# A two-layer Hyena and SSD trunk: weight loads and fresh stores issued from ScalarE's queue from layer 1 on

## The chip, the cores and the metric

The kernel runs on one core of a Trainium2 chip. The metric is the device time of one execution in microseconds (us). TensorE (PE) does the matrix products, VectorE (DVE), ScalarE (ACT) and GpSimd (POOL) the rest; SyncE (SP) only issues DMAs. A DMA can be issued from SP's, ACT's or POOL's instruction stream, and each of these streams is carried out in order.

## The reference

The input x is 1024 steps by 1024 channels, float32. Each layer computes h = LayerNorm(sqrt(2) h + mixer(h)). Layer 0's mixer is a bidirectional Hyena convolution. Layer 1's is a bidirectional Mamba-2 scan (SSD), cut to what matters:

```python
proj = x @ w_in                                  # z 2048, x B C 3072, dt 64 columns
xbc = silu(centred_depthwise_conv(xbc, conv_w, conv_b))          # 5 taps
# forward and backward, in 4 groups of 8 heads and 8 chunks of 128 steps:
states = einsum('bcsgn,bcghs,bcsghp->bcghpn', B, decay_states, x * dt)
y = y_diag + einsum('bctgn,bcghpn,bcght->bctghp', C, prev_states, exp(a_cs))
y = rms_norm_groups(y * silu(z), norm_g, 4)
return y @ w_out                                 # 2048 x 1024
```

## The kernel before, in words

Products are made in three parts: every operand is split into a high part h and a rest l, and H.H + H.L + L.H are added up in PSUM. So every weight tile is loaded to `wr`, cast by ACT to `wh` (L214, or L217 with a gain per row), and subtracted by DVE to `wl` (L215, L218). `weights` (L206 to L219) does these three; its load, at L211, is issued from SP. There are two `wr` tiles in the pool for the whole program, so the third load waits until DVE has made `wl` of the first; in layer 0's output projection the odd rows have two more of their own.

The stages in order of time:

- Layer 0's mixer, up to some 1120 us: projections at L261, the filters' and the signal's transforms.
- Layer 0's output projection (`out_layer`, products at L1193), up to some 1285 us, in passes of 2, 3 and 3 blocks of 128 rows of time; each pass reads all 16 rows of blocks of `w_out` (512 KB each) and y from DRAM (`yr`, L1175, split to `yh` and `yl`). It begins beside the end of the mixer; its first four groups of two rows of `w_out` are emitted there.
- Layer 1's projections (`flow` in `ssd`, products at L743), 40 units of 128 channels, with one `w1` load of 512 KB each, prepared in the middle of the unit before. A unit of x, B or C goes through `conv5` (ACT at L668, DVE four times at L671, Silu by ACT at L673) to a tile `cv`, and then through `ssd_xbc`: B and C are stored as they are (L961, 8 stores), x and B are transposed by PE (L969), copied by ACT to `tr` (L971, two tiles) and stored (L974, 40 stores), all to the DRAM tensor `bxd`.
- Layer 1's scan, from some 1400 us on, beside the projections. `ssd_back` takes the chunks of a group backwards, `ssd_forth` forwards one group later. Both load a chunk of B, C and x from `bxd` to `bx` (L983, three tiles), and the decays `ec` (L1017), each row of which is spread over 64 partitions. PE's first product of a chunk is at L1043, its last that reads `bx` at L1085. `ssd_back` stores its part to `ybd` (L1091), `ssd_forth` loads that (L1109), finishes y and stores it (L1147). In the last group, `values` (L1005) puts these tiles where h1^T lay (`h1th`, `h1tl`).
- Layer 1's output projection, like layer 0's, from some 2010 us to the end. Its early groups run beside the scan's last chunks. In its passes of three blocks, eight pairs of `wh` and `wl` are held, so that casts can run ahead.

What sets the order: the source emits the work as interleaved generators (`Pipe`, `fill`, `advance`), and the tile framework then writes a list for each engine when the program is built. It takes, on each engine, the instruction that its plan finds ready and that stands first in the source, so a list is near to the source's order but not the same. On the chip every engine carries out its list in order and waits at each instruction on semaphores, a DMA issue too: for its tile to be free, for the data that it stores, and for an earlier DMA that counted on the same semaphore.

The weight load and the stores of `ssd_xbc` before the change:

```python
# weights
nc.sync.dma_start(out=wr if len(src.shape) == 2 else ..., in_=src)          # L211
nc.scalar.copy(wh, wr)
nc.vector.tensor_tensor(out=wl, in0=wr, in1=wh.bitcast(F32), op=ALU.subtract)
# ssd_xbc
nc.scalar.copy(o, ps)                                                       # o is tr
nc.sync.dma_start(out=dst[:, c, n:n + 128], in_=o)                          # L974
```

Of the kernel before, what the change touches and what calls it, by code (L numbers as in the profile page):

```python
"""Hybrid encoder trunk, two layers on one core: a bidirectional Hyena layer, then a bidirectional
Mamba-2 SSD layer, each with its DeepNorm residual.

Matrix products run on float32r operands: each float32 operand is split into a high part of 12
significant bits and the rest (x = H + L), and a product is H.H + H.L + L.H in float32 PSUM.

Hyena's long convolution is evaluated at the 1024 points z_g = exp(-2 pi i (g + 1/4) / 1024). With
z^1024 = -i the products of a real signal and a two-sided real kernel wrap into the imaginary part,
so one complex transform of length 1024 gives the linear convolution of length 2048. The transform
is two stages (64 x 16) of matrix products, with t = 16 t1 + t2 and g = g1 + 64 g2.  # L10
"""
# [16 lines left out]
L = 1024  # L28
# [60 lines left out]
def _round12(a):  # L89
    """float64 -> float32 values with 12 significant bits, nearest even."""  # L90
    m, e = np.frexp(a)
    return np.ldexp(np.rint(m * 4096.0), e - 12).astype(np.float32)
# [40 lines left out]
def _constants():  # L133
    k = {}
# [3 lines left out]
    # both parts side by side, the high one first where n2 is even  # L138
# [34 lines left out]
class Pipe:  # L173
    """Tasks under way, each a generator that yields between its stages; a step moves each by a stage."""
# [15 lines left out]
class Build:  # L190
    def __init__(self, tc, a, p, pp, dp):
        """p, pp, dp: pools in SBUF (weights' tiles), PSUM and DRAM for the whole program."""
        self.tc, self.nc, self.a, self.p, self.pp, self.dp = tc, tc.nc, a, p, pp, dp
        self.ident = p.tile([128, 128], F32, name="ident")
        self.nc.sync.dma_start(out=self.ident, in_=a["ident"])
        self.ready = lambda k: True
        self.mhalf = p.tile([128, 1], F32, name="mhalf")
        self.nc.vector.memset(self.mhalf, -0.5)
# [7 lines left out]
    def weights(self, src, gain=None, pool=None, bufs=2, name="w"):  # L206
        """128 x 1024 (or 512) weights in two parts, times a gain per row if there is one."""
# [3 lines left out]
        nc.sync.dma_start(out=wr if len(src.shape) == 2 else wr.rearrange("p (k c) -> p k c", k=src.shape[1]), in_=src)  # L211
# [10 lines left out]
    def split(self, src, h, l):  # L222
        """h + l = src, both float32r."""
        self.nc.scalar.copy(h, src)  # L224
        self.nc.vector.tensor_tensor(out=l, in0=src, in1=h.bitcast(F32), op=ALU.subtract)  # L225

    def pair(self, pool):
        """The two parts' tiles of [128, 512] values."""
        return pool.tile([128, 512], F32R, name="xh", bufs=XB), pool.tile([128, 512], F32R, name="xl", bufs=XB)

    def load_pair(self, pool, src):
        """[128, 512] values from DRAM in two parts."""
# [12 lines left out]
    def load_r(self, pool, name, shape, src):  # L245
        """A float32r tile from float32 values that have 12 significant bits."""
# [4 lines left out]
    def projections(self, work, ahead, xh, xl):  # L251
        """Projections of x^T, each [128 channels, 1024] in PSUM for its function; a step per quarter of one."""
# [17 lines left out]
    def filter_mlp(self, pm, hs):  # L270
        """The filter network's last hidden layer at 16 n1 + n2 and at 1024 - (16 n1 + n2), in two parts on top of
        each other."""
# [45 lines left out]
    def filters(self, kd, sh, t):  # L318
        """The convolution kernels' transforms, to kd[block][re/im][64][16][256]; yields the tasks of each step."""
# [3 lines left out]
        def stage2(cb, j):  # L323
            # the last of the first stage's results go to DRAM two steps after their task's first
# [17 lines left out]
        with tc.tile_pool(name="k0", bufs=1) as p:  # L342
# [5 lines left out]
            with tc.tile_pool(name="k1", bufs=1) as p:  # L348
# [19 lines left out]
                def stage1(cb, m, k):  # L368
                    """The kernels at n2 = 2 m and 2 m + 1, and their transforms' first stage."""
# [42 lines left out]
    def hyena(self, yt, after):  # L412
        """Layer 0's mixer up to its output projection: from x^T (permuted time) to y^T in DRAM."""
# [4 lines left out]
        with tc.tile_pool(name="h0", bufs=1) as p, tc.tile_pool(name="hf", bufs=1, space=PSUM) as self.pf:  # L418
# [17 lines left out]
            for n, s in (("ta", [128, 16, 128]), ("tb", [128, 128]), ("tbi", [128, 128])):  # L436
                for q in "hl":
                    t[n + q] = (pa if n + q == "tah" else p).tile(s, F32R, name=n + q)
                    flat = t[n + q].rearrange("p a b -> p (a b)") if len(s) == 3 else t[n + q]
                    if n == "ta":  # L440
                        # not before x
# [5 lines left out]
            def u_work(b):  # L447
                """x1 * v for 256 channels."""
# [9 lines left out]
            def q_work(b):  # L458
                """x0 * silu(z) for 256 channels."""
# [14 lines left out]
            def fill(n):  # L474
                """Projections up to n quarters in all."""
# [23 lines left out]
            with tc.tile_pool(name="h1", bufs=1) as pf:  # L499
# [19 lines left out]
                for i, item in enumerate(todo):  # L519
                    if tabs and i == tabs[0][0]:  # L520
                        # a table's load waits for the products under way
# [41 lines left out]
    def hyena_fft(self, sh, t, us, spill, pb2):  # L563
        """A quarter of the first stage of the transform of 256 channels, to DRAM."""
# [34 lines left out]
    def hyena_mid(self, sh, p, t, kd, b, spill, vspill, j):  # L599
        """The transform's second stage, its product with the filters', and the inverse's first, to DRAM."""  # L600
# [29 lines left out]
    def hyena_back(self, sh, p, t, yt, b, vspill, qs, gs, pb2):  # L630
        """A quarter of the inverse's second stage times qs, to yt in the order of time."""
# [44 lines left out]
    def ssd(self, h1t, wdt, yt, after):  # L676
        """Layer 1's mixer up to its output projection: from h1^T to the normed y^T in DRAM; the first steps of what
        comes after are taken beside its last chunks."""
        tc, nc, a = self.tc, self.nc, self.a
        with tc.tile_pool(name="s", bufs=1) as p, tc.tile_pool(name="sf", bufs=1, space=PSUM) as self.pf:  # L680
# [10 lines left out]
            # the exponents' factors: in each direction, rows of ones (2), of the columns' terms (16)  # L691
            # against rows of the sums (2), and of the heads' places (16); odd chunks in the lower half
# [9 lines left out]
            # whether y^T's rows k, k + 1 are in DRAM for the first blocks  # L702
# [6 lines left out]
            # B, C, B^T and x at each chunk  # L709
# [19 lines left out]
            def flow():  # L729
# [7 lines left out]
                def column(ps, w, k, halves):  # L737
                    """What one k adds to 128 channels."""
# [5 lines left out]
                # the first two go through the first half of the time, then through the second  # L744
# [33 lines left out]
            def fill(n):  # L778
                """The order's units up to n quarters in all."""
# [18 lines left out]
            with tc.tile_pool(name="sc", bufs=1) as self.ps:  # L798
# [9 lines left out]
                def places(g):  # L808
                    """The group's rows of the exponents' factors."""
# [13 lines left out]
                for n in range(4):  # L823
# [4 lines left out]
                    else:  # L828
                        # the projections' input has been read
# [26 lines left out]
    def ssd_dt(self, p, h1t, t, wdt):  # L856
        """dt, the chunks' running sums of dt * a in both directions, and what follows of them."""
# [6 lines left out]
        # the second half of the time lies below the first: 64 heads x 512 steps each  # L864
# [32 lines left out]
        def columns(src):  # L897
            """[128, 2, 4, 64]: the heads along each row of the chunks."""
# [48 lines left out]
        def spread(c):  # L947
            """The chunk's exp(running sums) to DRAM, its heads of a parity together."""
# [7 lines left out]
    def ssd_xbc(self, p, t, g, b, v):  # L956
        """The group's B, C (b = 0, 1) or 128 channels of x, to DRAM in the forms that the scan takes."""
        nc = self.nc
        dst = t["bxd"][g].rearrange("c p n -> p c n")
        if b < 2:  # L960
            nc.sync.dma_start(out=dst[:, :, 128 * b:128 * b + 128], in_=v.rearrange("p (c n) -> p c n", n=128))  # L961
# [3 lines left out]
        for hf in range(2):  # L965
# [8 lines left out]
            nc.sync.dma_start(out=dst[:, c, n:n + 128], in_=o)  # L974

    def heads(self, v, g, c, d):
        """[128, 8, 64]: the group's head values at the chunk, along each head's channels."""
# [8 lines left out]
    def ssd_weigh(self, p, t, g, c, d, xs):  # L986
        """What each step's x adds to the state at the chunk's end: decay * dt * x."""
# [4 lines left out]
    def ssd_update(self, p, t, g, c, d, state, bc, xw):  # L992
        """The state after chunk c: S * exp(total) + B^T xw."""
# [11 lines left out]
    def values(self, pool, name, bufs, g, c, n=512):  # L1005
        """A tile of [128, n] values; in the last groups' chunks one in the place of the projections' input."""
# [6 lines left out]
    def ssd_decay(self, p, t, g, c, d):  # L1013
        """[128, 4, 128]: exp(running sum) at the chunk's steps, beside each head's channels."""
# [329 lines left out]
```

## Time and profile before

| | |
|---|---|
| runs | 2263.41, 2263.80, 2261.83 us; median 2263.41 |
| profiled execution | span 2258.7 us from its first to its last instruction; no other time of it is given; 4.7 us under the median |
| busy | PE 96%, weight loads into PE 74%, DVE 71%, ACT 52%, POOL 15% |
| DMA | 399 MB, 177 GB/s on average, all but 6 MB from SP's queue |

PE's busy time is modelled from pipelined products. A wait is put down to the release that came last. "SPq" marks what SP's queue issues and the time an issue takes; "PEclk" is the granted clock of TensorE as a share of full speed.

### The profile page before, as it was taken

To read this page: it belongs to the slowest core of one execution; us is meant where nothing else is said; L and a number is where in the kernel's file an instruction comes from. 1 tells how busy PE (TensorE), PEld (TensorE's weight loads), DVE (VectorE), ACT (ScalarE), POOL (GpSimd) and SP (SyncE) were. 2 spreads that over 40 slices of the span, in tenths; PEclk is the share of its full clock that TensorE was granted. 3 is DMA by queue.
4 is the path that set the end of the run, shared out by engine and by line. 5 is a ranking of instruction groups with operands and counts; after the bars stand their busy time and mean duration, and the time that the engine had idled before them with its cause. 6 is when DMAs were issued, how large, how long until landed. Compare 5 with 4: busy or idle time off the path is not lost.

```text
span 2258.7 us, 28866 instructions
## 1 busy us (share of the span) xinstructions
PE 2161.1 (96%) x9930; PEld 1676.8 (74%) x9930; DVE 1596.6 (71%) x2269; ACT 1172.2 (52%) x1688; POOL 333.5 (15%) x390
## 2 busy tenths in 40 slices
PE   8999999999999999999999997999999998887897
PEld 5677677878787878778777776777777776565686
DVE  7888877676766768657866564764876877765665
ACT  4677775455655555446654343645455555333442
POOL 0000000000000000000000102333344445534000
PEclk9999999999999999999999998999999999888999
DMA  6266778565656556557686425434455455446863
GB/s 201 100 216 229 238 250 258 174 195 159 188 156 177 167 161 177 149 167 207 232 303 202 147 64 156 124 110 127 142 153 163 154 150 166 147 156 197 265 218 128
DMA packets 261423, 399.26 MB, mean 177 GB/s; under 512 B 31879, under 2 KB 158599, under 8 KB 260765
## 3 DMA queue, kind: packets, MB, share of 16 engines
q1 hardware_dynamic: 247677, 391.38, 55.6%
q0 software_dynamic: 13600, 6.04, 1.2%
q8 instruction: 79, 1.29, 0.2%
q14 instruction: 67, 0.55, 0.1%
HBM read 280.64 MB, written 116.65 MB: 176 GB/s over the span
## 4 chain that ended last, share of the span: by engine, by line
PE 80%; DMA 9%; DVE 6%; ACT 2%; issue 2%; POOL 1%; SPq 0%; POOLq 0%; DVEq 0%; ACTq 0%
PE pj L261 31%; PE pj L743 16%; PE pj L1193 5%; PE pk L1193 5%; PE f L241 3%; PE f L242 3%; PE f L243 3%; DMA wr<-l_w_out 3%; DMA bx<-bxd 2%; PE f L1024 2%; PE f L1085 1%; PE f L996 1%; PE f L590 1%; PE f L1059 1%; PE f L376 1%
## 5 line engine op out<-in xcount | busy, mean ns | idle before, releaser
L261 PE MATMUL pj<-xth,wh 128*128 128x512 f32 x1024 | 329.3, 400 | 1.8 <-ACT xth L224 1.8
L261 PE MATMUL pj<-xtl,wh 128*128 128x512 f32 x1024 | 328.5, 398 | 1.4 <-DVE xtl L225 1.4
L261 PE MATMUL pj<-xth,wl 128*128 128x512 f32 x1024 | 325.6, 395 | 0.0
L215 DVE TENSOR_TENSOR wl<-wr,wh 128x1024 fp32r<-128x1024 f32 x152 | 192.1, 1266 | 153.0 <-ACT wh L214 151.3
L214 ACT CAST wh<-wr 128x1024 fp32r<-128x1024 f32 x152 | 159.5, 1049 | 190.0 <-PE pj L261 60.7
L261 PEld LDWEIGHTS pj<-xtl,wh 128*128 128x128 f32 x1024 | 192.3, 189 | 48.7 <-issue 4.6
L261 PEld LDWEIGHTS pj<-xth,wl 128*128 128x128 f32 x1024 | 192.2, 188 | 46.7 <-issue 4.6
L261 PEld LDWEIGHTS pj<-xth,wh 128*128 128x128 f32 x1024 | 188.6, 189 | 45.1 <-issue 3.8
L743 PE MATMUL pj<-h1th,wh 128*128 128x512 f32 x640 | 217.3, 413 | 0.9 <-DVE cv L671 0.9
L743 PE MATMUL pj<-h1th,wl 128*128 128x512 f32 x640 | 207.0, 400 | 0.0
L743 PE MATMUL pj<-h1tl,wh 128*128 128x512 f32 x640 | 206.9, 401 | 0.0
L225 DVE TENSOR_TENSOR xl<-bs,xh 128x512 fp32r<-128x512 f32 x192 | 129.2, 686 | 60.3 <-ACT xh L224 59.2
L1241 POOL TENSOR_SCALAR rs<-mv 128x1 f32<-128x1 f32 x16 | 8.3, 518 | 1019.8 <-DMA wr<-l_w_out 740.3
L224 ACT CAST xh<-bs 128x512 fp32r<-128x512 f32 x192 | 117.5, 620 | 67.5 <-PE f L642 29.0
L743 PEld LDWEIGHTS pj<-h1th,wh 128*128 128x128 f32 x640 | 118.8, 192 | 40.5 <-issue 18.6
L743 PEld LDWEIGHTS pj<-h1tl,wh 128*128 128x128 f32 x640 | 122.2, 192 | 28.4 <-issue 2.7
L743 PEld LDWEIGHTS pj<-h1th,wl 128*128 128x128 f32 x640 | 122.5, 193 | 27.2 <-issue 1.4
L559 DVE SCALAR_TENSOR_TENSOR cv<-pj,cw,cv 128x960 f32<-128x960 f32 x192 | 139.2, 744 | 4.8 <-ACT cv L556 2.7
L671 DVE SCALAR_TENSOR_TENSOR cv<-pj,cw,cv 128x1023 f32<-128x1023 f32 (+1 forms) x96 | 122.5, 1276 | 6.2 <-ACT cv L668 5.7
L1193 PE MATMUL pj<-wh,yh 128*128 128x512 f32 x320 | 105.5, 411 | 16.9 <-ACT wh L217 9.3
L1193 PE MATMUL pj<-wl,yh 128*128 128x512 f32 x320 | 104.5, 406 | 2.5 <-DVE wl L218 2.0
L1193 PE MATMUL pj<-wh,yl 128*128 128x512 f32 x320 | 102.8, 403 | 0.0
(264 smaller groups left out, 4226.2 us busy)
## 6 DMA issues: line engine op xcount, KB each, us to landing
wr<-w SPq DMA_DIRECT2D x104, 512.0 KB
wr<-l_w_out SPq DMA_DIRECT2D x96, 512.0 KB
k<-kd SPq DMA_DIRECT2D x256, 128.0 KB
ask<-asb SPq DMA_DIRECT2D x64, 256.0 KB
bs<-ask SPq DMA_DIRECT2D x64, 256.0 KB
kd<-asb SPq DMA_DIRECT2D x64, 256.0 KB
as<-asb SPq DMA_DIRECT2D x64, 256.0 KB
bs<-as SPq DMA_DIRECT2D x64, 256.0 KB
```

What stands on the lines that cost most here:

```text
L214: nc.scalar.copy(wh, wr)
L215: nc.vector.tensor_tensor(out=wl, in0=wr, in1=wh.bitcast(F32), op=ALU.subtract)
L224: self.nc.scalar.copy(h, src)
L225: self.nc.vector.tensor_tensor(out=l, in0=src, in1=h.bitcast(F32), op=ALU.subtract)
L241: mm(out, ah, bh, start=start, stop=False)
L242: mm(out, ah, bl, start=False, stop=False)
L243: mm(out, al, bh, start=False, stop=stop)
L261: self.nc.tensor.matmul(ps[:, t], lhs[:, k], rhs[:, k, t], start=st, stop=sp)
L559: nc.vector.scalar_tensor_tensor(out=acc[:, o], in0=ps[:, i], scalar=cw[:, w:w + 1], in1=acc[:, o], op0=ALU.mult, op1=ALU.add)
L671: nc.vector.scalar_tensor_tensor(out=acc[:, o], in0=ps[:, i], scalar=cw[:, w:w + 1], in1=acc[:, o], op0=ALU.mult, op1=ALU.add)
L743: nc.tensor.matmul(ps[:, c], lhs[:, k], rhs[:, k, c], start=st, stop=sp)
L1193: nc.tensor.matmul(po[hf], lhs[:, t], rhs[:, c], start=s, stop=e)
```

## The change

`Build` gets a queue `wq` for weights, SP's at first. `trunk` sets it to ACT's queue once layer 0's mixer and the load of dt's weights have been emitted, so before the rest of layer 0's output projection. All later weight loads are then issued from ACT's stream. The two stores of `ssd_xbc`, whose data ACT has just written, are issued from ACT's stream too. Comments and docstrings are taken out, each line staying as a blank one; nothing else differs.

```diff
 class Build:
         self.ready = lambda k: True
+
+        self.wq = self.nc.sync
...
     def weights(self, src, gain=None, pool=None, bufs=2, name="w"):
-        nc.sync.dma_start(out=wr if len(src.shape) == 2 else wr.rearrange("p (k c) -> p k c", k=src.shape[1]), in_=src)
+        self.wq.dma_start(out=wr if len(src.shape) == 2 else wr.rearrange("p (k c) -> p k c", k=src.shape[1]), in_=src)
...
     def ssd_xbc(self, p, t, g, b, v):
         if b < 2:
-            nc.sync.dma_start(out=dst[:, :, 128 * b:128 * b + 128], in_=v.rearrange("p (c n) -> p c n", n=128))
+            nc.scalar.dma_start(out=dst[:, :, 128 * b:128 * b + 128], in_=v.rearrange("p (c n) -> p c n", n=128))
...
             nc.scalar.copy(o, ps)
             c = slice(4 * hf, 4 * hf + 4)
             n = 128 * b + (128 if b else 256)
-            nc.sync.dma_start(out=dst[:, c, n:n + 128], in_=o)
+            nc.scalar.dma_start(out=dst[:, c, n:n + 128], in_=o)
...
 def trunk(tc, a, out):
         with tc.tile_pool(name="ht", bufs=1) as p:
             wdt = [w.rearrange("p (k c) -> p k c", k=8) for w in b.weights(a["wdt"], None, p, 1, "dw")]
             b.ht = p
+            b.wq = tc.nc.scalar
             h1t += [p.tile([128, 8, 1024], F32R, name=f"h1t{q}") for q in "hl"]
             for _ in mid:
                 pass
```

## Rows read from the trace of the kernel before

**Rows 1.** The page: PE's busy time, and the chain that ended last.

```profile
PE 2161.1 (96%) x9930; PEld 1676.8 (74%) x9930; DVE 1596.6 (71%) x2269; ACT 1172.2 (52%) x1688; POOL 333.5 (15%) x390
PE 80%; DMA 9%; DVE 6%; ACT 2%; issue 2%; POOL 1%; SPq 0%; POOLq 0%; DVEq 0%; ACTq 0%
```

**Rows 2.** Busy time by stage: length, engines, granted clock, DMA engines' busy share, GB/s.

```profile
core 0: us, PE busy (x) PEld busy (x) DVE busy (x) ACT busy (x) POOL busy (x), PEclk, DMA share, GB/s
1130.00:1285.00 155.00, 152.77 (x678) 122.55 (x677) 96.03 (x126) 65.36 (x78) 6.41 (x12) 1.00 0.64 219
...
1360.00:1440.00 80.00, 67.41 (x320) 52.18 (x318) 47.70 (x54) 37.43 (x47) 25.12 (x34) 0.91 0.52 149
1440.00:1880.00 440.00, 436.05 (x2269) 338.33 (x2268) 312.83 (x440) 227.67 (x293) 176.35 (x191) 1.00 0.47 142
1880.00:2004.00 124.00, 107.15 (x551) 76.65 (x550) 90.69 (x153) 47.07 (x75) 67.60 (x72) 0.89 0.47 143
2004.00:2131.00 127.00, 96.02 (x376) 71.20 (x376) 75.04 (x106) 43.66 (x55) 34.17 (x35) 0.88 0.70 220
```

**Rows 3.** Whom PE waited for, 1880 to 2004, then 2004 to 2131: us, times, longest.

```profile
PE f L1043 <- DMA bx<-bxd: 16.6, 7, 6.4
...
PE pj L1193 <- ACT wh L217: 9.3, 5, 3.3
PE f L1144 <- ACT rs L1141: 5.6, 5, 2.8
PE pj L1193 <- ACT yh L224: 5.5, 1, 5.5
```

**Rows 4.** Whom SP's queue waited for, 1280 to 2130: us, times, longest.

```profile
SPq L211 <- DVE wl L215: 129.9, 34, 12.7
...
SPq L974 <- ACT tr L971: 52.1, 14, 8.8
...
SPq L961 <- ACT cv L673: 47.1, 7, 11.4
...
SPq L1109 <- DMA y<-h1th: 23.7, 4, 6.5
```

**Rows 5.** Issues, of wr from 1112 on, of tr, cv: count, ns min/median/max, first and last.

```profile
L211 SPq DMA_DIRECT2D wr<-l_w_out x88: 327/332/2862, 1112.8 to 2220.1; - x88
...
L211 SPq DMA_DIRECT2D wr<-w x40: 327/333/4037, 1264.2 to 1882.3; - x40
...
L974 SPq DMA_DIRECT2D bxd<-tr x40: 360/407/2789, 1358.9 to 1873.8; - x40
L961 SPq DMA_DIRECT2D bxd<-cv x8: 365/372/425, 1325.7 to 1765.5; - x8
```

**Rows 6.** Timelines of ACT, SP, the chain and PE, 1386 to 1407: start, duration.

```profile
1389.29 1.07 ACT L971 COPY tr<-f 128x512 f32<-128x512 f32 x2 [0.74 <-PE f L969]
...
1386.83 1.11 SPq L1017 DMA_DIRECT2D ec<-ecd  x2
1388.00 4.04 SPq L211 DMA_DIRECT2D wr<-w  x1
1392.13 3.35 SPq L974 DMA_DIRECT2D bxd<-tr  x2
...
1392.70 10.88 DMA bxd<-tr
1403.59 3.10 DMA bx<-bxd
...
1407.04 0.76 PE L1043 MATMUL f<-bx 128*128 128x128 f32 x2 [10.50 <-DMA bx<-bxd]
```

**Rows 7.** The chain from 2004 to 2131 by line; weight loads' issues (SP) and casts (ACT).

```profile
by line: DMA wr<-l_w_out 37.7%; issue 8.7%; DVE wl L218 7.1%; DMA y<-h1th 6.7%; DMA h1th<-ecd 6.6%; DMA yr<-y 6.4%; ACT wh L217 5.5%; POOL ss L1139 2.4%; DMA h1th<-ybd 2.2%; POOL h1th L1124 1.7%; DVE st L1237 1.6%; DVE res L1236 1.5%; DVE h
...
2033.87 0.51 SPq L1017 DMA_DIRECT2D h1th<-ecd  x1
2034.48 2.86 SPq L211 DMA_DIRECT2D wr<-l_w_out  x1
...
2047.78 1.15 ACT L217 ACTIVATE wh<-wr,gain 128x1024 fp32r<-128x1024 f32 x1 [2.05 <-DMA wr<-l_w_out]
...
2092.99 0.35 SPq L211 DMA_DIRECT2D wr<-l_w_out  x1
...
2096.42 1.15 ACT L217 ACTIVATE wh<-wr,gain 128x1024 fp32r<-128x1024 f32 x1 [1.06 <-DMA wr<-l_w_out]
```

**Rows 8.** Whom ACT waited for, 2004 to 2131, then 1440 to 1880; the casts' durations (ns).

```profile
ACT yh L224 <- DMA yr<-y: 18.4, 5, 5.3
...
ACT L673 <- DVE cv L671: 49.1, 15, 7.0
ACT cbs L1045 <- PE f L1043: 41.9, 18, 7.0
...
L217 ACT ACTIVATE wh<-wr,gain x48: 1135/1152/1157, 2014.9 to 2223.7; 128x1024 fp32r<-128x1024 f32 x48
```

**Rows 9.** The chain's last products, and ACT's timeline in layer 0's output projection.

```profile
2228.05 16.33 PE pk L1193 x72
...
1218.59 1.04 ACT L214 CAST wh<-wr 128x1024 fp32r<-128x1024 f32 x1
1219.53 0.82 ACT L224 CAST yh<-yr 128x768 fp32r<-128x768 f32 x1
```

## The prediction

> **What bounds it now.** I read the page of the profile first. TensorE (PE) is busy 96% of the span, and the chain that ended last is 80% PE and 9% DMA [rows 1], so the change can win only where PE stands still, and only behind the switch of queues. The table by stages shows where that is [rows 2]. From 1440 to 1880 us PE is busy 436.05 of 440 us at full clock: nothing can be won there, only lost. From 1360 to 1440 it is busy 67.41 of 80, from 1880 to 2004 107.15 of 124, from 2004 to 2131 96.02 of 127; from 2131 it runs full again. Next, who PE waits for [rows 3]. Between 1880 and 2004 it is the load of a chunk of B, C and x (tile bx) at L1043, 16.6 us in 7 waits. The longest wait of the whole second layer, 10.50 us, is for the same tile, but at 1407, when the scan starts. Between 2004 and 2131 it is the cast of output weights (9.3 us), a cast of y (5.5), the norm's scale (5.6) and smaller ones.
>
> Last, SP's own waits [rows 4]: from 1280 to 2130 it stood 129.9 us in 34 waits for VectorE's wl before a weight load, and 52.1 and 47.1 us for ScalarE's (ACT's) tr and cv before their stores. Whatever followed on SP's queue stood behind them. The change takes exactly these waits off SP.
>
> **What moves.** The weight loads issued from 1112.8 on are 88 of w_out and 40 of w1 [rows 5]: 40 of layer 0's 48 rows of w_out (8 were emitted before the switch), 40 blocks of w1, 48 rows of layer 1's w_out. Stores: 40 of tr and 8 of cv [rows 5]. That is 176 DMAs. No arithmetic, byte or tile changes; SP and POOL keep all other DMAs.
>
> **Term A, the start of the scan (1388 to 1407): -6 us.** The last two tr tiles are copied from 1389.29 on and ready by 1390.4. SP is then inside the issue of a weight load, which takes it from 1388.00 to 1392.04, behind two ec loads begun at 1386.83. The two stores are issued from 1392.13 to 1395.48; the chain gives 10.88 us of store, and the bx loads go out at 1403.59 and take 3.10; PE resumes at 1407.04 [rows 6]. From ACT the stores go out right behind the copies, some 0.4 us each [rows 5], so by 1391.2, and not behind the ec loads in the same queue. Landing lies between the 3.43 us of an undisturbed 512 KB load [rows 7] and the 10.88 seen. I take 6.3, nearer the undisturbed end because the queue's head is free but the ec loads still move: landed at 1397.5 instead of 1403.6, 6 us sooner, and the bx loads follow. Bounds: nothing gained, or the whole stall of 10.5.
>
> **Term B, 1880 to 2004: 0.** Only the last weight loads lie there; the bx loads that PE waits for stay on SP behind ec loads and stores that stay too. It needs no cover: nothing is added to that path.
>
> **Term C, the turn into the last projection (2004 to 2131): -9 us.** Weight loads make 37.7% of the chain in this stretch, 47.9 of 127 us, in 7 pieces [rows 7]. A load that follows an ec load by 0.6 us is cast 13.30 us after its issue (2034.48 to 2047.78); one with none ahead is cast 3.43 us after it (2092.99 to 2096.42) [rows 7]. SP also stands 23.7 us in 4 waits for a y store before it may reload that tile [rows 4]. At 3.43 each the 7 pieces would be 24.0 us, so 23.9 are excess. I take less than half of it, because yr and ec stay on SP's queue behind those waits, and ACT waits 18.4 us for yr there [rows 8]: what is late next is yr. Bounds: nothing, or 23.9.
>
> A rule is weighed here apart from the sum. The Trainium skill ("DMA: Bandwidth & Descriptors", section "Queues, rings and completion order") says that SP and ACT own one ring each on every DMA engine, that descriptors start in ring order, and that an engine takes turns between rings by packet. By that rule a weight load would pass waiting ec loads, and C would lie at its upper bound; no row here shows a second such queue at work.
>
> **Term D, what ACT pays: +3 us.** An issue took SP 0.33 us for weights and 0.41 for tr, the worst 4.04 [rows 5]: 128 x 0.33 + 48 x 0.4 = 61 us on ACT. From 1440 to 1880 ACT is busy 227.67 of 440 us [rows 2], and much of its idle time is waiting for VectorE and PE (49.1 and 41.9 us are the largest) [rows 8], which covers issues. A wait for wl, 3.8 us each on SP, now holds up the copies and casts queued behind it on ACT, and through them VectorE, POOL's share of the mask and PE's transposes. PE's cover is that weights are cast a whole unit ahead and that PSUM has two banks for projections; I let one delay of 3 us through. Between 1130 and 1285 PE is busy 152.77 of 155 us [rows 2], with the same cover. Bounds: below nothing is excluded (ACT gains no work); above, the rival.
>
> **Sum.** -6 + 0 - 9 + 3 = -12 on the profiled span of 2258.7, which gives 2246.7; that span stands 4.7 under the median of the runs, 2263.4, so the prediction is 2251.4.
>
> **Rivals.** (1) *Slower: ACT's order lets only one weight load fly.* In the source each issue is followed by the cast that needs it. If ACT's list keeps that order, load i+1 goes out behind cast i, and a row of w_out costs 0.33 + 3.43 + 1.15 (cast [rows 8]) = 4.9 us, where SP keeps two in flight. It decides where PE wants rows faster than that: in passes of three blocks a row is 18 products at 16.33 / 72 = 0.227 us, 4.1 us [rows 9]. The excess of 0.8 us falls on 32 rows in layer 0's last two passes and some 24 after 2131: 45 us at most, half of it covered by the tiles cast ahead. With A kept this is +22 - 6, 2279; without a gain, 2285. Against it: the lists are not in source order. At 1218.59 ACT casts a weight and only then the yh of that group [rows 9], so an issue can stand well ahead of its cast. Chance 0.22, and then mostly in part, some +10 to +16.
>
> (2) *Nothing moves.* The stalls are made of bytes and of other DMAs: bx behind ec at 1403 and 1880 to 2004, yr behind ec after 2004, all of them left on SP, and what a weight load gains in its own queue it takes from the loads beside it. The DMA engines are busy 0.70 of 2004 to 2131 [rows 2], so there is not much room. SP's 61 us of issue time bounds nothing. A and C shrink to 2 us each, D eats them: 2262 to 2264. The Trainium skill (same page, section "Issuing engines are not separate DMA queues") says just that: DMAs of all issuers run on the same 16 engines, and a second issuer saves only sequencer time. Against it stands the 13.30 against 3.43 us, a wait in line and not of bytes [rows 7]. Chance 0.18.
>
> (3) *Both stalls go whole*: -10.5 - 23.9, 2229. PE's clock would add to it: granted 0.88 from 2004 to 2131 against 1.00 in the full stage [rows 2], one of its two levels being 1.2 and the other 2.4 GHz. Chance 0.05, because yr and ec stay where they are.
>
> (4) The change misses its words in one point: it begins in layer 0's last projection already. There PE does not wait, so this alters no number.
>
> **How the numbers follow.** A measurement of this kernel can tell about 0.2%, 4.5 us. Forecast (gains of 5 to 24 us) 0.55 and rival 3 0.05: faster 0.60. Rival 2: same 0.18. Rival 1: slower 0.22. The range 2231 to 2275 runs from all but the last of rival 3 to rival 1 in part; left out are the rest of both. The forecast's own range is 2239 to 2259.
>
> **What would show it.** A: PE's wait at the first L1043 falls from 10.5 to about 4.5 us, and the tr stores land in 6 us or so. C: PE busy over 2004 to 2131 rises, and weight loads beside ec loads are cast in well under 13 us after issue. D: PE stays at 99% between 1440 and 1880, and ACT's waits before issues are short. Rival 1 shows as PE waiting for wh in the passes of three blocks, with one load in flight; rival 2 as the same waits at the same tiles. The prediction is wrong if PE's idle time does not fall between 1388 and 2131, or if new waits for ACT stand in the full stages.

## The result and the profile after

The changed kernel takes 2297.8 us (median of 4 runs) against 2263.0 of the kernel before in the same comparison: ratio 1.0156, 95% interval 1.0141 to 1.0171, 35 us slower. The profiled execution took 2299.8 us, with a span of 2298.0.

The page after, busy time and chain, against [rows 1]: PE is 20.5 us longer busy for the same work, and the chain has lost 7 points of PE to DMA, DVE and ACT.

```profile
PE 2181.6 (95%) x9930; PEld 1683.9 (73%) x9930; DVE 1599.3 (70%) x2269; ACT 1169.3 (51%) x1686; POOL 329.9 (14%) x390
...
PE 73%; DMA 13%; DVE 7%; ACT 3%; issue 2%; POOL 1%; SPq 1%; ACTq 0%; POOLq 0%; DVEq 0%
```

The table by stages after, columns as in [rows 2]:

```profile
core 0: us, PE busy (x) PEld busy (x) DVE busy (x) ACT busy (x) POOL busy (x), PEclk, DMA share, GB/s
1130.00:1285.00 155.00, 148.47 (x654) 118.31 (x654) 91.39 (x116) 63.44 (x76) 6.14 (x10) 1.00 0.65 222
1360.00:1440.00 80.00, 70.51 (x302) 53.71 (x302) 44.17 (x48) 38.78 (x50) 24.24 (x32) 0.89 0.48 134
1440.00:1880.00 440.00, 428.47 (x2171) 328.83 (x2171) 295.30 (x421) 213.82 (x276) 161.17 (x178) 0.98 0.45 135
1880.00:2004.00 124.00, 106.66 (x544) 75.50 (x539) 95.01 (x148) 50.09 (x78) 67.58 (x71) 0.92 0.51 157
2004.00:2131.00 127.00, 95.78 (x432) 72.84 (x432) 72.55 (x107) 42.24 (x59) 44.57 (x46) 0.84 0.54 169
```

The two stages that were full have holes now: 148.47 of 155 us where it was 152.77, and 428.47 of 440 where it was 436.05, with the clock granted at 0.98 instead of 1.00. Of the stages that were to win, the first is fuller by 3.1 us, though with 302 products in it instead of 320; the other two are not. (The windows are fixed stretches of time; the changed kernel comes to the same work later, by the last table of this section.) PE's waits from 1090 to 2300 (us, times, longest), against [rows 3]:

```profile
PE f L1045 <- DMA bx<-bxd: 18.3, 8, 5.4
PE f L1146 <- ACT rs L1143: 11.6, 5, 5.5
PE f L1138 <- POOL dwh L1134: 10.0, 3, 6.9
PE f L971 <- ACT cv L675: 8.5, 4, 7.0
PE pj L1195 <- ACT yh L226: 7.2, 2, 5.6
PE pk L1195 <- issue: 4.9, 1, 4.9
```

The wait for the weights' cast (wh) is not among the first any more, but its place is taken by others, and only one of them, for the conv (cv), is at a tile whose DMA was moved. SP's waits from 1280 to 2130, against [rows 4]: the waits for wl, tr and cv are gone, and SP waits instead for the buffers of bx, y and ec.

```profile
SPq L985 <- PE f L1087: 191.9, 28, 18.6
SPq L1149 <- DVE y L1147: 108.9, 21, 10.1
SPq L1019 <- DVE y L1028: 107.6, 28, 16.3
```

How late the same piece of work starts, in us against the profiled execution before (from the start times in the traces). The last two columns are two kernels told of below, which take the change apart:

```
work (start before)                         after   queues alone   lists alone
a cast of weights, before the change (1104)  +1.1        +1.1          -0.4
last casts of layer 0's projection (1286)    +8.0        +3.8          +4.8
scan, chunk 2 (1421)                         +4.1        +8.5          +0.6
scan, chunk 16 (1697)                       +14.2       +12.0          +4.6
scan, chunk 19 (1757)                       +26.8       +13.3         +12.3
scan, chunk 32 (1990)                       +28.7       +14.4         +15.1
casts of the last projection (2126)         +33.6       +17.6         +17.8
statistics of the last rows (2245)          +39.3       +18.2         +23.4
```

More than half, 22.7 of the 39.3 us, is lost between 1421 and 1757, where the kernel before had hardly a hole. The columns end 2 to 5 us above the losses that the medians give (34.8, 15.1 and 21.7 us): the profiled execution before was a quick one, and single executions of one kernel differ by some 3 us at such a place, so only larger steps are read here.

### The profile page after: what moved, and what is told of

It is laid out like the page before. It is cut to its first block, busy times and chain, and to the rows that moved or that the text cites. A ratio compares the mean times of both kernels' runs of the same rounds, so it can differ in the third digit from the quotient of the medians.

```text
span 2298.0 us, 28756 instructions
## 1 busy us (share of the span) xinstructions
PE 2181.6 (95%) x9930; PEld 1683.9 (73%) x9930; DVE 1599.3 (70%) x2269; ACT 1169.3 (51%) x1686; POOL 329.9 (14%) x390
## 4 chain that ended last, share of the span: by engine, by line
PE 73%; DMA 13%; DVE 7%; ACT 3%; issue 2%; POOL 1%; SPq 1%; ACTq 0%; POOLq 0%; DVEq 0%
PE pj L263 30%; PE pj L745 15%; DMA wr<-l_w_out 4%; PE pj L1195 3%; PE f L243 3%; PE f L244 3%; PE f L245 3%; DMA bx<-bxd 2%; PE pk L1195 2%; PE f L1026 2%; PE f L998 1%; PE f L1061 1%; PE f L592 1%; PE f L1087 1%; DMA y<-h1th 1%
## 5 line engine op out<-in xcount | busy, mean ns | idle before, releaser
L1195 PE MATMUL pj<-wh,yh 128*128 128x512 f32 x320 | 104.5, 410 | 13.7 <-ACT yh L226 7.2
L1074 POOL TENSOR_TENSOR m<-m,dm 128x512 f32<-128x512 f32 x64 | 87.9, 1374 | 99.5 <-DVE m L1066 96.1
```

The lines of the kernel that those rows point to most:

```text
L1074: nc.gpsimd.tensor_tensor(out=m, in0=m, in1=dm, op=ALU.add)
L1195: nc.tensor.matmul(po[hf], lhs[:, t], rhs[:, c], start=s, stop=e)
```

## The experiments

**One part at a time.** Each is the changed kernel with all but one part taken back.

```diff
 stores alone          -            b.wq = tc.nc.scalar
 layer 0's rows alone  +            b.wq = tc.nc.sync      (ahead of b.ssd; stores on SP)
 w1 alone              b.wq = tc.nc.scalar ahead of b.ssd, nc.sync ahead of rest.close(); stores on SP
 layer 1's rows alone  +                        self.wq = nc.scalar   (ahead of rest.close(); stores on SP)
```

> Only the 48 stores (tr, cv) are issued from ACT; all weight loads stay on SP. Theory 1 (a weight load issued from ACT stands behind ACT's own waits, and ACT's casts and copies stand behind the wait of the issue for the buffer): the stores follow the copy that ACT has just made, so they wait for nothing; the scan starts 2 to 5 us earlier, no loss between 1440 and 1880, 2258 to 2263. Theory 2 (the stores carry the loss, by the late copies of cv and tr that DVE waits for in the scan): 15 to 25 us lost between 1440 and 1880, 2278 to 2288. Theory 3 (neither queue matters; the loss comes from the new order that each edit gives the lists of all engines): no part carries what it is said to carry; some -5 to +10 anywhere behind 1290.

> Only the 40 weight loads of layer 0's output projection are issued from ACT. Theory 1: the whole loss of the stage before 1300 is here, +7 to +9 (2270 to 2272), with PE's waits for wh and wl between 1112 and 1180 as in the changed kernel, and nothing behind. Theory 2: as theory 1 for this stage, since no store moves here. Theory 3: the loss here is not +8 but anything from 0 to 10, and other stages move too although nothing of theirs is changed.

> Only the 40 weight loads of layer 1's input projections (w1) are issued from ACT. Theory 1: these carry the loss of 1440 to 1880, +15 to +25 (2278 to 2288), with ACT's waits for wl before issues and PE's waits behind ACT's late casts and copies. Theory 2: no loss, 2260 to 2265. Theory 3: in between, with PE's waits at bx loads that SP issues later than before, and not at tiles of ACT.

> Only the 48 weight loads of layer 1's output projection are issued from ACT. Theory 1: loss in the passes of three blocks behind 2131 and little before, +5 to +12 (2268 to 2275). Theory 2: 2263 to 2267. Theory 3: -5 to +12 with the loss not at wh or wl. The prediction's term C would have this part alone at 9 below the kernel before, 2254.

Measured: stores 2275.5 (ratio 1.0061, 1.0044 to 1.0078), layer 0's rows 2268.5 (1.0029, 1.0020 to 1.0039), w1 2265.0 (1.0011, 1.0002 to 1.0021), layer 1's rows 2273.3 (1.0049, 1.0033 to 1.0065), against 2261.8. The losses of 13.7, 6.7, 3.2 and 11.5 make 35.1, as much as the whole; but each of these kernels was built with lists of its own, so they are not shares of it. Every part loses, and the w1 loads, which theory 1 held for the loss in the scan, least. The stores lose most, and theory 1 had said that they wait for nothing; theory 2 came nearer. For layer 1's rows theory 1 had the size, for layer 0's the 6.7 us lie just under its 7 to 9. Layer 1's rows, by term C 9 us of gain, are 11.5 of loss. In the stores' trace the loss is at one place. Of SP's queue, stores alone, 1712 to 1718:

```profile
1714.20 0.31 SPq L985 DMA_DIRECT2D bx<-bxd  x1
1714.92 0.32 SPq L1093 DMA_DIRECT2D ybd<-y  x1
1716.00 0.51 SPq L1019 DMA_DIRECT2D ec<-ecd  x1
1716.62 0.47 SPq L985 DMA_DIRECT2D bx<-bxd  x1
```

The second bx load stands 0.6 us behind an ec load. Its packets end 8.8 us after its issue; PE's longest wait from 1630 to 1810 is for it:

```profile
PE f L1045 <- DMA bx<-bxd: 3.7, 1, 3.7
```

In the kernel before the same two loads are issued at 1709.92 (bx) and 1710.33 (ec), and the bx ends 4.0 us after its issue. Nothing of these two was changed: the build plans the lists of all engines anew when a DMA changes its queue. In the changed kernel the pair stands in the wrong order too (ec 1724.39, bx 1725.00, landed after 8.7 us).

**The pair turned back.** The stores from ACT as above, with one edge that puts that ec load (and one more in the next group) behind the bx load; all else stays, list by list.

```diff
+        with self.tc.issue_after(self.loads[-4]) if d == 0 and c == 2 and g in (1, 2) else ExitStack():
             self.nc.sync.dma_start(out=ec.rearrange("p i n -> p (i n)"), in_=src)
```

> The stores alone from ACT, as in the first experiment, and in SP's list two neighbours changed back, at two places: the load of a chunk (bx) again ahead of the load of ec that stood 0.6 us in front of it (1716.6 and 1892.5 us in that experiment). Nothing else differs from it. Theory of the order (the loss of 9 us around 1697 to 1757 is this one bx load, 8.8 us from issue to landing behind the ec load where others take 3.5 to 5.3, and the half clock after it): that bx lands in 3.5 to 5.5 us, PE does not wait for it, and the kernel gains 6 to 9 us on the first experiment, 2266 to 2269. Theory of the queue (stores from ACT delay ACT's other work, whatever SP's order): 2273 to 2277 as before, with the loss at the same chunks.

Measured: 2269.1 (1.0031, 1.0020 to 1.0042), 6.4 us less than with the stores alone. SP's queue from 1719 to 1722:

```profile
1719.87 0.31 SPq L985 DMA_DIRECT2D bx<-bxd  x1
1720.60 0.32 SPq L1094 DMA_DIRECT2D ybd<-y  x1
1721.13 0.32 SPq L985 DMA_DIRECT2D bx<-bxd  x1
1721.68 0.51 SPq L1020 DMA_DIRECT2D ec<-ecd  x1
```

The bx now ends 4.5 us after its issue, and PE does not wait for it. Two pairs of neighbours in a list of 1309 DMAs were worth 6 us. The stores were also tried from POOL, without and then with these edges (`nc.gpsimd` in both stores):

> The 48 stores from POOL's queue, weights on SP. On ACT they cost 13.7 us. If the loss was ACT's (its copies and activations stand behind the wait of a store's issue for an older DMA, 11.45 us at 1372 to 1383 in the first experiment) it goes: 2258 to 2266. If it comes with taking the stores off SP at all, by the order of what is left on SP, 2270 to 2277. Against both: POOL has work of its own in the scan (a third busy), and a store waiting there for a copy delays it: up to +10 on either.

> The 48 stores from POOL's queue, as in the ninth experiment (2264.0), and in SP's list the two bx loads again ahead of the ec loads; all other lists as there. In that experiment's trace the scan's first chunk came 1 to 4 us sooner than before and 8 us were lost at the chunks of 1717 and 1738, where PE waited 4.2 us for the bx load that stands behind an ec load. Theory of the order: those 6 to 8 us come back, 2256 to 2259, 0.1 to 0.3% under the kernel before. Rival (the wait comes with the other buffers' turns, whatever the order): 2263 to 2265.

Measured: 2264.0 (1.0011, 1.0001 to 1.0020) and 2261.6 (1.0001, 0.9993 to 1.0010, 5 rounds). From POOL the stores leave the lists of PE, DVE and ACT almost as they were (33, 9 and 2 places hold another instruction, against 198, 129 and 63 from ACT), and cost almost nothing. With the edges the kernel is as fast as the one before, not faster: 2261.6 lies between the two theories, and its 2.4 us are not clear of noise, since the two intervals overlap. What the order is worth is shown by the stores from ACT alone.

**The loads of the output projections, in other ways.** If the loads are late because their issue stands behind ACT's own waits, POOL's empty queue must heal it, and so must an earlier place in ACT's list.

```diff
 from POOL   b.wq = tc.nc.gpsimd, self.wq = nc.gpsimd (both projections; w1 and the stores on SP)
 ahead       wr of both rows issued first, then
+                    with tc.issue_after(self.issued):
+                        self.split(yr, yh, yl)
```

> The output projections' weight loads of both layers (88 rows) from POOL's queue instead of ACT's; w1 and the stores on SP as in the kernel before. Theory of the line on ACT (a load's issue stands behind ACT's own waits for other loads, so only one flies at a time): POOL has no work and no waits in these stretches, so the 7 us before 1150 and the 12 us behind 2004 that the two experiments on ACT lost together (2268.5 and 2273.3) are not lost: 2255 to 2265. Rival (two queues share the DMA engines and the loads are late for that): both losses stay in part, 2270 to 2282. If the prediction's term C was right but for ACT's line, 2250 to 2256.

> The output projections' weight loads of both layers from ACT, but in ACT's list the cast of a group's y stands behind the issue of that group's two weight loads instead of ahead of it. Theory of the line on ACT: the wait of the cast for yr (3.8 us at 1131) no longer holds back an issue; of the 18 us that these loads lost from ACT (7 and 12 alone), a third to two thirds come back, 2267 to 2275; the casts of the weights themselves still stand ahead of later issues. Rival: no gain, 2279 to 2283.

Measured: 2279.2 (1.0073, 1.0057 to 1.0089) and 2280.1 (1.0077, 1.0060 to 1.0093). Both rivals' numbers, 17 to 18 us lost either way. The lists were planned anew here too, so this does not yet tell the queue from the lists.

**Queues and lists crossed.** A table of the order of the kernel before (or of the changed one) is put in, and an edge without a semaphore from each instruction to the next holds each engine's list to it. Only the 176 moved DMAs find their own place.

```diff
+        for each engine's list, name after name:
+            tc.add_manual_dep(made[name], before, mybir.DependencyInfo(NoSync, DATA))
 queues alone: DMAs as in the change, lists of the kernel before
 lists alone:  DMAs as in the kernel before, lists of the change
```

> The whole change (176 DMAs on ACT), but with edges that hold the lists of all engines to those of the kernel before: every matmul, every operation of DVE, ACT and POOL, and SP's remaining 1181 DMAs in the order that they have there; only the moved DMAs find their own place in ACT's list. Theory of the lists (the loss comes mostly from the new order that the build gives all engines, 744 places of PE's list among them, not from who issues): 2255 to 2270. Theory of the queue (the loads and stores are late, and ACT's work behind them, because of where they are issued): 2285 to 2300.

> The reverse: all DMAs issued as in the kernel before (weights and stores on SP), but the lists of PE, DVE, ACT and POOL and the order of SP's other DMAs held to those of the changed kernel. Theory of the lists: the loss comes with them, 2285 to 2300. Theory of the queue: 2258 to 2270. If both parts matter, the two crossed kernels' losses add up to about the 35 us.

Measured: queues alone 2279.0 (1.0062, 1.0046 to 1.0079), lists alone 2285.6 (1.0093, 1.0078 to 1.0108), against 2263.9: 15.1 and 21.7 us, together 36.8. Both theories were half of it: 2279.0 lies in neither range, 2285.6 just inside what the theory of the lists gave for them. With the lists alone, every DMA issued as before, the wrong pair is there again, and so is PE's wait (SP's queue from 1714, and PE's waits from 1640 to 1760):

```profile
1714.75 0.51 SPq L1019 DMA_DIRECT2D ec<-ecd  x1
1715.37 0.41 SPq L985 DMA_DIRECT2D bx<-bxd  x1
...
PE f L1045 <- DMA bx<-bxd: 3.3, 1, 3.3
```

With the queues alone the pair is right, and the step of 8 to 13 us between chunks 16 and 19 is 1.3 us.

**What the queues cost.** With the lists held to those of the kernel before, first the stores are put back:

> The 128 weight loads on ACT, the stores back on SP, all engines' lists held to those of the kernel before. With the stores on ACT too it was 2279 (15 above before). Theory of the store's wait (on ACT a store stands behind a DMA issued eight earlier, an ecd store of SP, and everything of ACT behind it: 11 us at the start of the scan): with the stores off ACT the 7 to 8 us between 1336 and 1434 are not lost, 2268 to 2273, and what is left is lost in the two output projections. Rival (the weight loads carry all of it): 2277 to 2281.

Measured: 2275.9 (1.0068, 1.0052 to 1.0083), 14.7 of the 15.1 us. The stores' own part is nothing that can be measured; the weight loads carry it. In the traces the start of the scan does win, as expected: from 1286 to chunk 3 this kernel loses 2.2 us, with the stores on ACT 7.7. But from chunk 32 to the casts of 2126 it loses 5.4 instead of 3.2, and the whole hardly moves. Then only the 88 rows of the output projections, from POOL, from ACT, and from ACT with 26 of them issued ahead of the cast of the row before:

> All lists held to those of the kernel before; only the 88 weight loads of the two output projections go, to POOL's queue, which has next to nothing to do there. Theory of the line on ACT (a load stands behind ACT's waits for other tiles): nothing is lost here, 2260 to 2266, while the same from ACT loses 10 to 15. Theory of the one order (on SP the loads of y, of the residual and of the weights start one after the other as they are needed; from two queues they share the DMA engines and the needed one comes late): the loss is the same as from ACT, 2270 to 2278.

> As the kernel with POOL, but the 88 loads on ACT. In the whole change with these lists the output projections lost 2 to 3 us (layer 0) and 4 to 10 (layer 1). Both theories: 2268 to 2276; it is the measure for the other two.

> As the kernel with the 88 loads on ACT, but 26 of them, 24 of these in layer 1, are issued ahead of the cast of the row before (they stood behind it), so that two loads fly. Theory of the line on ACT: a third or more of that kernel's loss comes back, 3 to 8 us less than it. Theory of the one order: within 2 us of it. If earlier loads only push back the loads of y, it is slower.

Measured: POOL 2273.5 (1.0055, 1.0040 to 1.0070), ACT 2271.6 (1.0046, 1.0031 to 1.0062), ACT early 2278.5 (1.0074, 1.0055 to 1.0093), against 2261.4. ACT's own waits alone can't be the cause: from POOL's queue as much is lost. (That POOL's queue has a price of its own instead was not excluded.) What is late for ACT is y. Its waits from 1990 to 2290 before, from ACT, from POOL, and early:

```profile
ACT yh L224 <- DMA yr<-y: 19.8, 7, 5.3
```

```profile
ACT yh L226 <- DMA yr<-y: 28.2, 7, 8.2
```

```profile
ACT yh L226 <- DMA yr<-y: 23.8, 5, 7.5
```

```profile
ACT wh L219 <- DVE wl L220: 23.8, 8, 6.7
ACT yh L226 <- DMA yr<-y: 20.3, 4, 8.7
```

The longest wait for yr grows from 5.3 to 8.2, 7.5 and 8.7 us. In the early kernel, an issue ahead of a cast also makes ACT stand 23.8 us for wl, which it must wait for before it may load; so its 7 us more need not come from loads that start sooner. The loads of y do take longer: the fourth, fifth and sixth of layer 1 are complete 10.0, 8.2 and 8.5 us after their issue before, 12.3, 10.7 and 10.1 with the weights from ACT, 13.2, 11.6 and 10.0 from POOL. But PE does not wait longer for yh: at most 5.5 us before, then 5.0, 4.5 and 4.3. What grows for PE is its wait for the norm's scale of the scan's last chunks, in the same four kernels:

```profile
PE f L1144 <- ACT rs L1141: 5.6, 5, 2.8
```

```profile
PE f L1147 <- ACT rs L1144: 8.3, 5, 3.7
```

```profile
PE f L1147 <- ACT rs L1144: 9.9, 5, 4.1
```

```profile
PE f L1147 <- ACT rs L1144: 9.3, 5, 4.3
```

How the loads of weights lead to this wait was not shown. Last, the loads of y and of the residual follow the weights to POOL's queue in SP's old order, or the loads of y go there alone:

```diff
+ one queue: yr and res also from self.yq = nc.gpsimd, held among themselves to SP's order
+ y alone:   only yr from nc.gpsimd
```

> All lists held to those of the kernel before; in the output projections the 88 loads of weights and with them 44 loads of y and 16 of the residual go from POOL's queue, held among themselves to the order that they had on SP. Theory of the split (two queues sharing the DMA engines): nothing is split, so the 4.5 us that weights from POOL alone lost in layer 0's projection (1104 to 1156) go, and most of the loss behind 1990; 2262 to 2268. In layer 1's first pass POOL has work of its own, and the stores of y that these loads wait for land late, so a few us may stay there. Theory of the issuer (any queue but SP costs, by its issue or its start): as the weights from POOL, 2271 to 2278, with the 4.5 us there again.

> All lists held to those of the kernel before; only the 44 loads of y go from POOL's queue, the weights stay on SP. Theory of the split: the same two streams are split as when the weights move, so about the same is lost, 2268 to 2275. Theory of the issuer: half as many DMAs move, and y is loaded two rows ahead, so 2262 to 2266. If SP's line was what delayed y, faster than before: 2254 to 2260.

Measured: 2268.6 (1.0033, 1.0021 to 1.0044) and 2264.4 (1.0007, 0.9997 to 1.0017), against 2262.4. With one order again, 148 DMAs on POOL lose 6.2 us where 88 lost 12.1 (the intervals just overlap), and in the traces 1.2 us where 4.3 were lost from 1104 to 1286; that speaks for the split, though 2268.6 is above what that theory gave. The loads of y alone lose 2.0, not clear of nothing, where the split foretold 6 to 13: a miss. The theory of the issuer gave 2262 to 2266 for that one and holds it, but it missed the kernel with one queue (2271 to 2278). So neither theory holds both. Nor are late loads of y the whole of it: with one queue the same three are complete after 5.7, 6.5 and 4.0 us, sooner than before, and half of the loss is still there. The reading that is left is that it is not any split that costs, but the weights, about two thirds of the bytes (88 of 512 KB, beside 44 of at most 384 and 16 of 512), running free of the order in which SP let them start. That is argued and not shown, and so is that the shares of the DMA engines are how it costs; the 6 us left with one queue stay open.

## Why the prediction was wrong

**The step that failed first** is "No arithmetic, byte or tile changes; SP and POOL keep all other DMAs": true, but the sum took it for granted that all other instructions also keep their order. They don't; in the built programs 744 of the 9292 places in PE's list hold another matmul. The lists alone cost 21.7 us. No term and no rival had them, and the range, 2231 to 2275, ended 23 us short. The queues alone cost another 15.1 us where the sum had them gain 12; there it is terms A and C that failed, as follows.

**Term A (-6)** had the sign, not the reason. Between 1286 and chunk 2 the changed kernel gains 3.9 us; by chunk 3, 13 us later, nothing is left of it (8.0 us late at 1286, 9.7 there). And the lists alone gain 4.2 up to chunk 2, while the queues alone lose 4.7. The stores do go out right behind the copies, as the term said; it is the copies that are late. ACT's list after, 1386 to 1407:

```profile
1386.83 0.93 ACTq L976 DMA_DIRECT2D bxd<-tr  x2
1387.86 0.65 ACTq L213 DMA_DIRECT2D wr<-w  x1
1388.55 1.06 ACT L675 ACTIVATE cv<-cv 128x1024 f32<-128x1024 f32 x1 [10.13 <-issue]
...
1405.40 1.07 ACT L973 COPY tr<-f 128x512 f32<-128x512 f32 x2 [0.75 <-PE f L971]
1406.01 0.93 ACTq L976 DMA_DIRECT2D bxd<-tr  x2
```

The last two copies come at 1405.40 where they came at 1389.29 [rows 6]. Ahead of them ACT stood 10.13 us, until two stores could be issued, while SP was inside the issue of eight ecd stores:

```profile
1372.90 13.74 SPq L953 DMA_DIRECT2D ecd<-dwh  x8
```

PE's wait of 10.5 us for bx is gone, but 7.0 us for cv (L971) stand in its place. What held the first of the two stores can be read in the trace: it counts on the same semaphore as an ecd store that SP issued at 1380.07. That one's last completion comes at 1386.76, and ACT's issue begins at 1386.83. So the store no longer stood behind other issues on SP, but it still stood behind a DMA of SP, which the term had at nothing.

**Term B (0)**: 1.9 us lost between chunks 19 and 32. It held.

**Term C (-9)** read its ground rightly: the 13.30 us from issue to cast [rows 7] were a load's time. The chain before has both pieces:

```profile
2034.48 13.27 DMA wr<-l_w_out
2047.78 1.16 ACT wh L217
```

By its semaphore, 14 of the load's 16 completions were in 6.0 us after its issue; the last two came at 13.2 and 13.3, right behind the last two of the ec load issued ahead of it. And the loads did get shorter: the third to twelfth of that projection are complete after 6.7 us on average in the changed kernel (6.9 with the queues alone, 8.2 with the lists alone), after 8.4 before. What failed is the price, 3.43 us each, and the step from there to PE, that the waits beside it stay as they were. The chain over the same work, 2032 to 2164 after:

```profile
by line: DMA y<-h1th 22.3%; DMA wr<-l_w_out 19.0%; DMA h1th<-ybd 12.0%; DMA h1tl<-bxd 7.3%; issue 6.7%; DVE wl L220 5.7%; POOL h1th L1126 3.6%; ACT wh L219 2.6%; POOL ss L1141 2.3%; POOL rs L1243 2.0%; DVE st L1239 1.9%; DVE yl L227 1.8%; P
```

Weight loads fell from 37.7% of it to 19.0, and the scan's stores of y and loads of ybd, which stay on SP, rose from 6.7 and 2.2% to 22.3 and 12.0. PE's longest waits in that stretch, and its wait for wh:

```profile
PE f L1146 <- ACT rs L1143: 10.8, 4, 5.5
PE f L1138 <- POOL dwh L1134: 7.6, 2, 6.9
...
PE pj L1195 <- ACT wh L219: 1.8, 2, 1.0
```

PE's wait for wh fell from 9.3 to 1.8 us, but that came with the lists: over the same work it is 2.4 with the lists alone and 7.6 with the queues alone. And the wait for rs rose from 5.6 to 10.8 (14.2 and 8.7 in those two). In all the stretch lost 4.9 us (1990 to 2126). That yr would be late next was right for ACT with the queues alone (29.5 us from 1990 to 2290, where it was 19.8), not in the changed kernel (10.5 us in this stretch, where it was 18.4).

The premise of the ring did hold. A weight load 1.8 us behind an ec load on SP (1911.99 before) was complete 10.0 us after its issue; the same row from ACT (1927.00, queues alone, 2.2 us behind the ec load) in 7.1. This is what the Trainium skill ("DMA: Bandwidth & Descriptors", "Queues, rings and completion order") says of rings taking turns. By that rule C would lie at its upper bound; it does not: the loads got shorter, but not to 3.43 us, and PE then waited for other things. The same page's section "Issuing engines are not separate DMA queues" says that a second issuer saves only sequencer time, the mechanism of rival 2; here it did not even come out at no change.

**Term D (+3)**: with the queues alone, chunks 3 to 24 lose 1.7 us (11.5 to 13.2). The size was right for what it counted. The lists alone lose 10.8 us there (1.6 to 12.4), and the change, with both, 17.1.

**Rival 1** had the sign and some of the size (45 us at most), not the mechanism. It priced one load in flight; with loads issued ahead of the cast before them the kernel is 7 us slower still (ACT then also waits for wl), and a queue without casts loses as much.

**Rival 4**, "there PE does not wait, so this alters no number", was wrong: layer 0's rows alone cost 6.7 us. In that kernel PE's waits for wh and wl at the start of the stage are 5.8 us (1104 to 1160), where they were 0.9 (1104 to 1150). The DMA engines were busy 0.9 to 1.0 of 1120 to 1150 before already; that this is why was not tested.

**What would show it**: the test that was to decide, PE's idle time between 1388 and 2131, did: by the tables it grew, most of all from 1440 to 1880, 4 to 11.5 us. The second sign, new waits for ACT in full stages, was only half the story: in the scan they are for bx and y.

## What to carry to other kernels

Where a build plans the lists, moving a DMA is never only that: compare the lists of all engines before and after, and hold them with edges to measure the queue alone. A queue's waits may be its worth: the reading that fits these runs best, though none shows it by itself, is that SP's line held the weights back until the loads that were needed first were on their way. Before the shortening of a wait is priced as a gain, look at what stands next on the same path: here it took the whole.

## What the runs showed of the hardware

A bx load 0.6 us behind an ec load takes 8.1 to 8.8 us to land (by its last packet) where its neighbours take 3 to 5, in three kernels, at two places in each. The semaphores show more of it. That of a bx load is updated sixteen times; that of an ec load, of 256 KB, only three times: 0.9 us after its issue, and then twice, 7.7 to 8.3 us after it (between 1431 and 1470 before). Of the bx load behind one (issued at 1716.62, stores alone), thirteen updates are in after 3.9 us, and the last two come after 8.9 and 9.5. It looks as if the ec load's bytes went through two of the DMA engines alone, and the part of the next load that goes through the same two had to stand behind them; no experiment tested that.

In these traces a hole costs more than itself: beside it and after it the clock is granted at its lower level. Over 1720 to 1760 with the stores alone PE was busy 35.5 of 40 us, at 0.83 and 0.91 of full clock:

```profile
1720.00:1740.00 20.00, 16.28 (x77) 12.47 (x75) 10.21 (x15) 5.49 (x8) 6.72 (x8) 0.83 0.30 88
1740.00:1760.00 20.00, 19.24 (x77) 14.27 (x77) 11.37 (x17) 10.91 (x15) 6.32 (x7) 0.91 0.58 178
```

In the changed kernel the time at half clock rose from 86 to 117 us: of the 39 us between the two profiled spans, up to 15.5 were PE at work at half speed, which its busy time counts as busy.
